# The first gate and up chunk of a SwiGLU taken together, product by product, in a decoder trunk on one core

## The chip, the cores and the metric

The kernel runs on one core of a Trainium2 chip. The metric is the device time of one execution in microseconds (us), lower is better. PE is the matrix engine, DVE the vector engine, ACT the scalar engine, POOL the general engine, SP the engine that issues most DMA transfers. PE has two clock levels, 1.2 and 2.4 GHz.

## The reference, cut to what matters

One decoder layer, float32, 1024 tokens of width 1024, hidden width 2816:

```
x += 1/2 * swiglu(rms_norm(x, ffn1_norm), w_gate, w_up, w_down)     # first FFN
x += mixer(rms_norm(x, mix_norm))                                   # GDN and Mamba heads, not touched
x += 1/2 * swiglu(rms_norm(x, ffn2_norm), w_gate, w_up, w_down)     # second FFN
out = rms_norm(x, final_norm)
swiglu(h) = (silu(h @ w_gate) * (h @ w_up)) @ w_down
```

## The kernel before

**A chunk.** The gate and up matrices are taken in chunks of 256 columns, 11 of each, in the order gate 0, up 0, gate 1, up 1 and so on. One chunk is the product of a 256 by 1024 weight block and the 1024 by 1024 normalised, transposed tokens. It is done by Strassen's scheme in Winograd's form: seven products (numbered 1 to 7) of half-sized operands instead of eight. Every operand is split into a rounded high part and a low rest, so each product is 4 slices of the contraction times three matmuls of 128x512 (L326 high by high, L327 high weights by low tokens, L328 low weights by high tokens): 12 matmuls a product, 84 a chunk.

**Weight operands** (`a_ops`). For each product DVE forms a sum or difference of two blocks (tile `as`, L305; products 3 and 4 need none), ACT rounds it (L235, tile `ah`) and DVE takes the rest (L236, tile `al`). One call makes up to four products into one pair of tiles, of which there are two; a third call waits until every matmul on the first pair has been issued and is done.

**Token operands.** Slices of the normalised tokens are transposed by PE (L212, tile `ps_sc`, two PSUM banks) and combined by DVE and ACT into the operand of each product, again with an ACT cast (L235, tile `bh`) and a DVE rest (L236, tile `bl`). The first 512 tokens (`x0`) give products 2 and 4 (`b_first`). The second 512 (`x1`) with kept copies of the first (`keepx`, called r11 and r21) give 3, 5, 1, 6 and 7 (`b_second`). `b_second` goes slice by slice: for each of four slices it makes all five operands, nine DVE instructions. Temporaries (`bs`, `as`, `raw`, and the copy `m3` of a product) share the tag `q`, four buffers.

**The order of the first two chunks** (`gate_up_all`). Products 2 and 4 of gate 0 and up 0 run first, since their token operands come first. Then the loop over chunks runs gate 0 (3, 5, 1, 7, 6), then up 0, then chunk 2 (gate 1) and so on. PSUM has eight banks: `pj` three, `mx` two, `sc` two, `oo` one. The products' sums are combined on DVE (L375 to L403) and the results written to DRAM (L424).

**What sets the order.** Within an engine the instruction order is fixed when the program is built: a planner goes through the instructions with their data dependences and its own estimate of durations, takes on each engine the earliest instruction in program order that is ready, and so lets later instructions fill gaps. `issue_after(ins)` forces the instructions of a block behind `ins` on that engine. On the chip each engine then runs its list in order.

**The start.** SP issues the first four token blocks (L615), the weight blocks of gate 0 and up 0 (L291) and the last four token blocks (L619). ACT's own DMA queue issues eight small loads of norm and convolution columns (`load_cols`, L96 to L102), which PE transposes and DVE copies into `cols`; the first scaling of tokens (L258) needs them. `normalise_pairs` computes mean squares and scales blocks 0 to 3 in pairs, one square on ACT and one on DVE; `normalise` does blocks 4 to 7 (L164 squares, L166 on the rest, L186 and L188 scaling). At the second FFN the same functions run behind the last output products of the mixer (L121 to L123, L1282).

## Time and profile before

| | |
|---|---|
| time, three runs | 2331.36, 2332.07, 2332.08 us (median 2332.07) |
| the profiled execution | 2332.2 us |
| its span, first to last instruction | 2330.5 us |
| mean granted PE clock | 0.996 |
| PE busy | 2283.3 us (98%) |
| DVE, ACT busy | 1724.9 us (74%), 1100.1 us (47%) |

The profiled execution is 0.1 us above the median of the runs and 1.7 us longer than its span. PE is busy nearly everywhere in the 40 slices of the page; the one low slice is the first (58 us a slice, six tenths). A busy PE can still be one that runs slowly or waits between matmuls, so stretches are read by their instructions.

### The profile page before, as it was taken

What the parts mean: (1) busy time and instruction counts of PE and PEld (TensorE: products, weight loads), DVE (VectorE), ACT (ScalarE), POOL (GpSimd) and SP (SyncE); (2) the same over time, 40 slices, a digit from 0 to 9 for tenths busy, and PEclk for the clock granted to TensorE, in tenths of its full rate; (3) what the DMA queues carried; (4) which work ended last, traced back from release to release, by engine and by line L of the source; (5) the groups of instructions that cost most, each with busy time, mean ns of one, the idle gap of its engine ahead of it and who ended that gap; (6) DMA issues with size and microseconds to landing.
All of it is one profiled execution on the core that took longest, in us unless ns stands there. A gap on an engine that the chain in (4) does not pass through costs nothing.

```text
span 2330.5 us, 31422 instructions
## 1 busy us (share of the span) xinstructions
PE 2283.3 (98%) x11734; PEld 1868.9 (80%) x11734; DVE 1724.9 (74%) x3347; ACT 1100.1 (47%) x1992; POOL 49.5 (2%) x117
## 2 busy tenths in 40 slices
PE   6999999999999999999999999999999999999998
PEld 3788888888878888888888888888778888888886
DVE  7876767667775675668778888778697777767687
ACT  6433333343367785873455556422543333334334
POOL 0000000000000010000000000000000000000000
PEclk9999999999999999999999999999999999999999
DMA  3332323484553322232332322335222333329456
GB/s 110 104 118 88 116 95 109 145 311 131 183 190 107 94 91 55 73 103 73 82 100 73 80 73 64 122 98 190 91 86 95 109 100 109 107 91 348 142 158 214
DMA packets 220967, 281.33 MB, mean 121 GB/s; under 512 B 46905, under 2 KB 153590, under 8 KB 219790
## 3 DMA queue, kind: packets, MB, share of 16 engines
q1 hardware_dynamic: 220548, 279.23, 37.2%
q8 instruction: 92, 1.51, 0.3%
q14 instruction: 61, 0.50, 0.1%
q10 hardware_dynamic: 266, 0.10, 0.0%
HBM read 211.55 MB, written 67.73 MB: 120 GB/s over the span
## 4 chain that ended last, share of the span: by engine, by line
PE 83%; DVE 9%; DMA 3%; ACT 3%; issue 2%; SPq 0%; POOL 0%; ACTq 0%; DVEq 0%
PE ps_pj L123 9%; PE ps_pj L121 9%; PE ps_pj L122 9%; PE ps_pj L327 7%; PE ps_pj L328 6%; PE ps_pj L326 6%; PE ps_mx L326 3%; PE ps_mx L327 3%; PE ps_mx L328 3%; PE ps_pj L485 2%; PE ps_pj L486 2%; PE ps_pj L484 2%; PE ps_oo L327 2%; PE ps_oo L326 2%; PE ps_oo L328 2%
## 5 line engine op out<-in xcount | busy, mean ns | idle before, releaser
L123 PE MATMUL ps_pj<-hhi,wlo 128*128 128x512 f32 x832 | 334.2, 402 | 0.0
L121 PE MATMUL ps_pj<-hhi,whi 128*128 128x512 f32 x832 | 332.9, 400 | 0.4 <-ACT gsb L744 0.4
L122 PE MATMUL ps_pj<-hlo,whi 128*128 128x512 f32 x832 | 332.1, 399 | 0.0
L326 PE MATMUL ps_pj<-bh,ah 128*128 128x512 f32 x704 | 276.0, 393 | 6.8 <-ACT bh L235 6.3
L327 PE MATMUL ps_pj<-bl,ah 128*128 128x512 f32 x704 | 276.8, 393 | 3.7 <-DVE bl L236 3.7
L328 PE MATMUL ps_pj<-bh,al 128*128 128x512 f32 x704 | 275.5, 392 | 0.0
L123 PEld LDWEIGHTS ps_pj<-hhi,wlo 128*128 128x128 f32 x832 | 156.7, 188 | 28.6 <-issue 0.7
L121 PEld LDWEIGHTS ps_pj<-hhi,whi 128*128 128x128 f32 x832 | 156.7, 188 | 28.6 <-ACT gsb L744 0.9
L122 PEld LDWEIGHTS ps_pj<-hlo,whi 128*128 128x128 f32 x832 | 156.7, 188 | 27.9
L326 PEld LDWEIGHTS ps_pj<-bh,ah 128*128 128x128 f32 x704 | 132.5, 189 | 38.8 <-ACT bh L235 11.5
L235 ACT CAST ah<-wst 128x512 fp32r<-128x512 f32 x88 | 54.9, 624 | 226.7 <-PE ps_oo L327 137.6
L327 PEld LDWEIGHTS ps_pj<-bl,ah 128*128 128x128 f32 x704 | 133.0, 189 | 34.5 <-DVE bl L236 7.3
L328 PEld LDWEIGHTS ps_pj<-bh,al 128*128 128x128 f32 x704 | 133.0, 189 | 27.3 <-DVE al L236 0.3
L235 ACT CAST hid<-hraw 128x1024 fp32r<-128x1024 f32 (+1 forms) x84 | 82.4, 983 | 143.1 <-PE ps_oo L486 62.8
L305 DVE TENSOR_TENSOR as<-wst 128x512 f32<-128x512 f32 x220 | 145.3, 685 | 3.7 <-DMA wst<-in_ffn_w_up_dram 2.7
L236 DVE TENSOR_TENSOR al<-as,ah 128x512 fp32r<-128x512 f32 x220 | 140.4, 685 | 0.0
L326 PE MATMUL ps_mx<-bh,ah 128*128 128x512 f32 x352 | 137.5, 393 | 1.7 <-ACT bh L235 1.5
L327 PE MATMUL ps_mx<-bl,ah 128*128 128x512 f32 x352 | 138.3, 393 | 0.7 <-DVE bl L236 0.7
L328 PE MATMUL ps_mx<-bh,al 128*128 128x512 f32 x352 | 137.8, 391 | 0.0
L235 ACT CAST ah<-as 128x512 fp32r<-128x512 f32 x220 | 124.3, 617 | 7.4 <-DVE as L305 7.1
L236 DVE TENSOR_TENSOR hid<-hraw,hid 128x1024 fp32r<-128x1024 f32 (+1 forms) x84 | 95.1, 1132 | 35.0 <-ACT hid L235 34.2
L335 ACT COPY m<-ps_pj 128x512 f32<-128x512 f32 x88 | 51.8, 588 | 129.5 <-PE ps_pj L328 129.5
(427 smaller groups left out, 5086.1 us busy)
## 6 DMA issues: line engine op xcount, KB each, us to landing
hraw<-hid_scr SPq DMA_DIRECT2D x70, 512.0 KB, 3.9
hid_scr<-hs SPq DMA_DIRECT2D x110, 256.0 KB, 2.4
wst<-in_ffn_w_down_dram SPq DMA_DIRECT2D x50, 512.0 KB, 4.7
wst<-in_ffn_w_gate_dram SPq DMA_DIRECT2D x22, 1024.0 KB, 5.6
wst<-in_ffn_w_up_dram SPq DMA_DIRECT2D x22, 1024.0 KB, 5.3
wst<-in_w_in_dram SPq DMA_DIRECT2D x36, 512.0 KB, 4.1
hid_scr<-sg SPq DMA_DIRECT2D x44, 256.0 KB, 2.0
keep<-in_ffn_w_down_dram SPq DMA_DIRECT2D x20, 512.0 KB, 6.2
```

Of the source, the lines that this page charges most:

```text
L121: T.matmul(o, lhsT=wh, rhs=mh, start=first, stop=False)
L122: T.matmul(o, lhsT=wh, rhs=ml, start=False, stop=False)
L123: T.matmul(o, lhsT=wl, rhs=mh, start=False, stop=last)
L235: A.copy(out=hi, in_=src)
L236: return V.tensor_tensor(out=lo, in0=src, in1=hi.bitcast(F32), op=ALU.subtract)
L305: V.tensor_tensor(out=t, in0=v[0], in1=v[1], op=v[2])
L326: T.matmul(bank, lhsT=wh[:, k], rhs=bh[:, k], start=a, stop=False, skip_group_check=True)
L327: T.matmul(bank, lhsT=wh[:, k], rhs=bl[:, k], start=False, stop=False, skip_group_check=True)
L328: T.matmul(bank, lhsT=wl[:, k], rhs=bh[:, k], start=False, stop=z, skip_group_check=True)
L335: A.copy(out=t, in_=bank)
L484: T.matmul(bank, lhsT=hh, rhs=wh, start=first and k == 0, stop=False, skip_group_check=True)
L485: T.matmul(bank, lhsT=hh, rhs=wl, start=False, stop=False, skip_group_check=True)
```

## The change

- `load_cols`: the eight small loads are issued by SP, behind the four token blocks and ahead of the weights, and not by ACT.
- `normalise_pairs`: the square of block 3 is taken on ACT. `a_start(0)` (products 2 and 4 of both chunks) is forced behind the last scaling of the first half on DVE.
- `b_first` no longer makes r21 (the scaled second half of `x0`).
- `a_second` goes. `a_start` makes the weight operands of gate 0 and up 0 together, in four calls: (2, 4), (3, 6), (7, 5), (1), the second one behind `normalise` of the second half.
- `b_second` goes product by product: 3 and 6 for each slice, then 7 (from a second transposing of `x0`), then 5, then 1, with the weight calls 2 and 3 between; r22 is kept.
- `gate_up_all` runs gate 0 and up 0 together: 2 and 4, then 3, 6, 7, 5, 1, each for both chunks, with sums combined in another order; the loop starts at chunk 2. Product 7 takes the two `sc` banks. Weights of gate 1 and up 1 are loaded behind the last weight call.

```diff
     def load_cols(pool):
-        nc.scalar.dma_start(out=st, in_=gdn_conv_w[0].rearrange("t (c p) -> (t c) p", p=P))
+        nc.sync.dma_start(out=st, in_=gdn_conv_w[0].rearrange("t (c p) -> (t c) p", p=P))
...
         for i in range(0, 4, 2):
             ss = pool.tile([P, 2], F32, name="ss")
             A.activation(out=junk[:, 0], in_=xt[i], func=AF.Square, accum_out=ss[:, 0:1])
-            V.scalar_tensor_tensor(out=junk[:, 1], in0=xt[i + 1], scalar=1.0, in1=xt[i + 1],
-                                   op0=ALU.mult, op1=ALU.mult, accum_out=ss[:, 1:2])
+            if i == 0:
+                V.scalar_tensor_tensor(out=junk[:, 1], in0=xt[1], scalar=1.0, in1=xt[1],
+                                       op0=ALU.mult, op1=ALU.mult, accum_out=ss[:, 1:2])
+            else:
+                A.activation(out=junk[:, 1], in_=xt[3], func=AF.Square, accum_out=ss[:, 1:2])
...
-            pt, w1 = transposed(x0, k + 4), wcol[:, k + 4:k + 5]
...
-            A.mul(out=r21[:, k], in_=pt, mul=w1)
...
+    def b_second(pool, x0, x1, wcol, H, r11, r22, between):
...
+        def scaled(pt, kx, other, op):
+            return lambda t: V.scalar_tensor_tensor(out=t, in0=pt, scalar=wcol[:, kx:kx + 1], in1=other,
+                                                    op0=ALU.mult, op1=op)
         for k in range(4):
...
+            A.mul(out=r22[:, k], in_=transposed(x1, k + 4), mul=wcol[:, k + 4:k + 5])
+            p12 = transposed(x1, k)
+            operand(3, k, scaled(p12, k, r22[:, k], ALU.subtract))
+            operand(6, k, scaled(p12, k, r11[:, k], ALU.add))
+        between(2)
+        for k in range(4):
+            operand(7, k, scaled(transposed(x0, k + 4), k + 4, r22[:, k], ALU.add))
+        for k in range(4):
+            split(b_op(H, 5)[0][:, k], b_op(H, 5)[1][:, k], r22[:, k])
+        between(3)
+        for k in range(4):
+            operand(1, k, lambda t: V.tensor_tensor(out=t, in0=r11[:, k], in1=r22[:, k], op=ALU.add))
...
+    A_START = (((0, 2), (0, 4), (1, 2), (1, 4)), ((0, 3), (1, 3), (0, 6), (1, 6)),
+               ((0, 7), (1, 7), (0, 5), (1, 5)), ((0, 1), (1, 1)))
+
+    def a_start(pool, raws, ops, n):
+        a_ops(pool, *((raws[j], m, ops[j]) for j, m in A_START[n]))
...
         for st in ops:
             open_bank(st, "c21", 2, pool.tile([P, 512], F32, name="m2f"))
             prod(st["c21"], st, 4, False)
+        for st in ops:
+            open_bank(st, "c12", 3, pool.tile([P, 512], F32, name="m3", tag="q"))
+        for st, tag in zip(ops, ("pj", "oo")):
+            open_bank(st, "c22", 6, None, tag)
+        for st in ops:
+            open_bank(st, "c11", 7, None, "sc")
...
+        for j, st in enumerate(ops):
+            q, pp = st["m3"], st["m2"]
+            V.tensor_tensor(out=q, in0=q, in1=pp, op=ALU.subtract)
+            V.tensor_tensor(out=pp, in0=st["c21"], in1=q, op=ALU.add)
+            gated(s21, st["c21"], j)
+            V.tensor_tensor(out=pp, in0=st["c11"], in1=pp, op=ALU.add)
+            st["m1"] = wtile(j == 0, "m1")
+            V.tensor_tensor(out=st["m1"], in0=st["c22"], in1=q, op=ALU.add)
+        for j, st in enumerate(ops):
+            prod(st["c12"], st, 5, False)
+            V.tensor_tensor(out=st["m2"], in0=st["m2"], in1=st["c12"], op=ALU.subtract)
+            gated(s12, st["c12"], j)
+        nxt = [{}]
+        for j, st in enumerate(ops):
+            open_bank(st, "c1", 1, None, "mx")
+            pp, r = st["m2"], st["m1"]
+            V.tensor_tensor(out=pp, in0=st["c1"], in1=pp, op=ALU.add)
+            V.tensor_tensor(out=r, in0=st["c1"], in1=r, op=ALU.add)
+            a_ops(pool, *((raws[0], m, nxt[0]) for m in A_GROUPS[j]))
...
+                V.tensor_tensor(out=s11, in0=pp, in1=s11, op=ALU.mult)
+                V.tensor_tensor(out=s22, in0=r, in1=s22, op=ALU.mult)
+                hid_store(work, scr, 0, s12, s22, s11, s21)
+        next_load()
         sg = None
         for i, (p, w) in enumerate(todo):
+            if i < 2:
+                continue
...
+    def start_rest(pool, w_gate, w_up, raws, ops):
+
+        def f(n):
+            a_start(pool, raws, ops, n)
+            if n == 3:
+                raws[:] = [a_load(w, 1) for w in (w_gate, w_up)]
+
+        return f
...
-            x0 = normalise_pairs(npool, xt, "h6")
-            a_first(npool, raws, ops)
-            keep = [kp.tile([P, 4, 512], F32, name=f"keepx{i}") for i in range(2)]
-            b_first(npool, x0, nrm[0], H, keep)
-            a_second(npool, raws, ops)
+            x0, last = normalise_pairs(npool, xt, "h6")
+            with tc.issue_after(last.ins):
+                a_start(npool, raws, ops, 0)
+            r11, r22 = (kp.tile([P, 4, 512], F32, name=f"keepx{i}") for i in range(2))
+            b_first(npool, x0, nrm[0], H, r11)
             x1 = normalise(1, npool, xt, jtag="h7")
-            b_second(npool, x1, nrm[0], H, keep)
+            a_start(npool, raws, ops, 1)
+            b_second(npool, x0, x1, nrm[0], H, r11, r22,
+                     start_rest(npool, ffn1_w_gate[0], ffn1_w_up[0], raws, ops))
...
-    a_first(npool, raws, ops)
-    a_second(npool, raws, ops)
+    a_start(npool, raws, ops, 0)
+    a_start(npool, raws, ops, 1)
...
-    b_second(npool, x1, nrm[2], H, keep)
+    b_second(npool, x0, x1, nrm[2], H, r11, r22, start_rest(npool, ffn2_w_gate[0], ffn2_w_up[0], raws, ops))
```

## Rows read from the trace of the kernel before

**Rows 1.** The page of the whole execution: busy time, share of the span and instructions of each engine; then the shares of the span by engine in the chain that ended last.

```profile
PE 2283.3 (98%) x11734; PEld 1868.9 (80%) x11734; DVE 1724.9 (74%) x3347; ACT 1100.1 (47%) x1992; POOL 49.5 (2%) x117
...
PE 83%; DVE 9%; DMA 3%; ACT 3%; issue 2%; SPq 0%; POOL 0%; ACTq 0%; DVEq 0%
```

**Rows 2.** Busy time of each engine in stretches around the second half of the token operands and behind it: stretch and length, then busy us (instructions) of PE, PEld, DVE, ACT, POOL, granted PE clock, DMA share, GB/s. The first two rows are the first FFN, the third is its steady run of chunks, the last is the second FFN.

```profile
41.30:63.70 22.40, 15.79 (x62) 9.21 (x60) 21.66 (x36) 14.81 (x26) 0.00 (x0) 0.92 0.00 1
63.70:86.12 22.42, 22.42 (x99) 18.43 (x99) 21.91 (x37) 12.47 (x21) 0.00 (x0) 1.00 0.36 118
104.00:150.00 46.00, 46.00 (x204) 38.10 (x203) 32.09 (x52) 15.93 (x29) 0.00 (x0) 1.00 0.33 109
1692.90:1706.55 13.65, 9.62 (x30) 5.17 (x28) 13.65 (x23) 9.26 (x16) 0.00 (x0) 0.72 0.00 0
```

**Rows 3.** PE's instructions in order of time: start, duration, line, output and inputs, shape, count, and in brackets the idle time before it and what ended it. The first matmul of the first FFN, the last one that waited in its first two chunks, the first one of chunk 2 and of chunk 2's product 2; then in the second FFN the first matmul of product 2, the first transposing of `x1`, and the first matmul of chunk 2.

```profile
21.66 1.22 PE L326 MATMUL ps_mx<-bh,ah 128*128 128x512 f32 x2 [0.43 <-ACT bh L235]
...
63.70 0.50 PE L327 MATMUL ps_pj<-bl,ah 128*128 128x512 f32 x1 [0.70 <-DVE bl L236]
...
83.40 0.39 PE L326 MATMUL ps_pj<-bh,ah 128*128 128x512 f32 x1
...
86.12 0.39 PE L326 MATMUL ps_mx<-bh,ah 128*128 128x512 f32 x1
...
1676.58 0.39 PE L326 MATMUL ps_mx<-bh,ah 128*128 128x512 f32 x1
...
1682.14 0.66 PE L212 MATMUL ps_sc<-ident,xt 128*128 128x128 f32 x4 [0.34 <-ACT xt L186]
...
1729.13 0.39 PE L326 MATMUL ps_pj<-bh,ah 128*128 128x512 f32 x1
```

**Rows 4.** DVE's instructions in order of time, same columns: the first of `b_second` and the first combining of sums behind it, in the first and in the second FFN.

```profile
42.03 0.75 DVE L279 SCALAR_TENSOR_TENSOR bs<-ps_sc,cols,raw 128x512 f32<-128x512 f32 x1 [2.08 <-ACT raw L277]
...
64.78 0.68 DVE L375 TENSOR_TENSOR m<-m,m2f 128x512 f32<-128x512 f32 x1
...
1684.46 0.75 DVE L279 SCALAR_TENSOR_TENSOR bs<-ps_sc,cols,raw 128x512 f32<-128x512 f32 x1 [2.12 <-ACT raw L277]
...
1706.59 0.69 DVE L375 TENSOR_TENSOR m<-m,m2f 128x512 f32<-128x512 f32 x1
```

**Rows 5.** The start: two rows of what SP's queue waited for (us in total, times, longest), the first and the last of the eight column loads on ACT's queue, SP's issue of gate 0's weights, ACT's first instruction, and PE's transposing of the last columns.

```profile
SPq L615 <- DMA xt<-in_x_dram: 3.0, 1, 3.0
SPq L615 <- DMA colst<-in_ssm_conv_b_dram: 1.1, 1, 1.1
...
0.81 0.42 ACTq L96 DMA_DIRECT2D colst<-in_gdn_conv_w_dram  x1
...
5.69 0.28 ACTq L102 DMA_DIRECT2D colst<-in_ffn_norm_dram  x1
...
6.54 0.43 SPq L291 DMA_DIRECT2D wst<-in_ffn_w_gate_dram  x1
...
6.00 1.28 ACT L197 ACT_TABLE_LOAD   x1 [6.00 <-DMA colst<-in_ssm_conv_w_dram]
...
8.46 0.39 PE L105 MATMUL ps_mx<-ident,colst 93*128 93x93 f32 x1 [3.41 <-DMA colst<-in_ffn_norm_dram]
```

**Rows 6.** Busy time of each engine in stretches of the start, columns as in rows 2.

```profile
12.00:21.00 9.00, 3.36 (x12) 1.98 (x12) 8.30 (x23) 5.46 (x9) 0.00 (x0) 1.00 1.00 362
...
21.00:28.00 7.00, 6.57 (x27) 5.22 (x26) 3.46 (x6) 6.36 (x13) 0.00 (x0) 1.00 0.01 4
28.00:34.00 6.00, 4.29 (x20) 2.52 (x18) 5.06 (x9) 6.00 (x13) 0.00 (x0) 1.00 0.01 1
```

**Rows 7.** DVE and ACT in order of time, first FFN: the square of block 1, first and last step of the first pair's inverse root, the square of block 3, the first weight cast, the scaling of block 2, the first scaling by a column, the first square of the second half and the start of its inverse root.

```profile
5.99 1.23 DVE L198 SCALAR_TENSOR_TENSOR junk<-xt 128x1024 bf16<-128x1024 f32 x1 [5.99 <-DMA xt<-in_x_dram]
...
8.47 0.17 DVE L201 TENSOR_SCALAR ssv<-ss 128x2 f32<-128x2 f32 x1 [1.25 <-ACT junk L197]
...
10.60 0.15 DVE L118 SCALAR_TENSOR_TENSOR rstd<-rs_t,rstd 128x2 f32<-128x2 f32 x1
...
11.24 1.23 DVE L198 SCALAR_TENSOR_TENSOR junk<-xt 128x1024 bf16<-128x1024 f32 x1 [0.50 <-DMA xt<-in_x_dram]
...
14.38 0.62 ACT L235 CAST ah<-wst 128x512 fp32r<-128x512 f32 x1 [2.46 <-DMA wst<-in_ffn_w_gate_dram]
...
17.30 1.15 ACT L204 ACTIVATE xt<-xt,rstd 128x1024 f32<-128x1024 f32 x1 [1.04 <-DVE rstd L118]
...
19.38 0.68 ACT L258 ACTIVATE keepx<-ps_sc,cols 128x512 f32<-128x512 f32 x1
19.96 1.04 ACT L164 ACTIVATE junk<-xt 128x1024 bf16<-128x1024 f32 x1
...
36.34 0.17 DVE L166 TENSOR_SCALAR ssv<-ss 128x4 f32<-128x4 f32 x1
```

**Rows 8.** One transposing of four blocks on PE, and the three steps of one operand of product 7 (DVE sum, ACT cast, DVE rest), first FFN, columns as in rows 3.

```profile
57.35 0.60 PE L212 MATMUL ps_sc<-ident,xt 128*128 128x128 f32 x4
57.44 0.68 DVE L285 TENSOR_TENSOR bs<-keepx,raw 128x512 f32<-128x512 f32 x1
...
58.20 0.61 ACT L235 CAST bh<-bs 128x512 fp32r<-128x512 f32 x1
...
59.30 0.68 DVE L236 TENSOR_TENSOR bl<-bs,bh 128x512 fp32r<-128x512 f32 x1
```

More of the change, by code (lines that the diff above doesn't have):

```diff
@@ L252, in b_op, with b_first @@
         return H[m]
-    def b_first(pool, x0, wcol, H, keep):
-        r11, r21 = keep
+    def b_first(pool, x0, wcol, H, r11):
         for k in range(4):
@@ L259, in b_first @@
             split(b_op(H, 2)[0][:, k], b_op(H, 2)[1][:, k], r11[:, k])
-            pt, w1 = transposed(x0, k + 4), wcol[:, k + 4:k + 5]
             t = pool.tile([P, 512], F32, name="bs4", tag="q")
-            V.scalar_tensor_tensor(out=t, in0=pt, scalar=w1, in1=r11[:, k], op0=ALU.mult, op1=ALU.subtract)
+            V.scalar_tensor_tensor(out=t, in0=transposed(x0, k + 4), scalar=wcol[:, k + 4:k + 5],
+                                   in1=r11[:, k], op0=ALU.mult, op1=ALU.subtract)
             split(b_op(H, 4)[0][:, k], b_op(H, 4)[1][:, k], t)
-            A.mul(out=r21[:, k], in_=pt, mul=w1)
-    def b_second(pool, x1, wcol, H, keep):
-        r11, r21 = keep
+    def b_second(pool, x0, x1, wcol, H, r11, r22, between):
         def operand(m, k, f):
@@ L308, in a_ops @@
             ops[m] = hi[:, i], lo[:, i]
-    def a_first(pool, raws, ops):
-        a_ops(pool, *((raws[j], m, ops[j]) for j in range(2) for m in (2, 4)))
-    def a_second(pool, raws, ops):
-        a_ops(pool, *((raws[0], m, ops[0]) for m in (3, 5, 1, 7)))
+    A_START = (((0, 2), (0, 4), (1, 2), (1, 4)), ((0, 3), (1, 3), (0, 6), (1, 6)),
+               ((0, 7), (1, 7), (0, 5), (1, 5)), ((0, 1), (1, 1)))
+    def a_start(pool, raws, ops, n):
+        a_ops(pool, *((raws[j], m, ops[j]) for j, m in A_START[n]))
     def gate_up_all(pool, H, w_gate, w_up, scr, raws, ops, work, tail):
         todo = [(p, w) for p in range(NF2) for w in (w_gate, w_up)]
-        loads = todo[2:]
+        loads = todo[4:]
         def prod(bank, ops, m, first):
@@ L336, in open_bank, with wtile, next_load @@
                 st[f"m{m}"] = t
-        nxt = ops
+        def wtile(gate, name):
+            return work.tile([P, 512], F32, name=name, tag="sg" if gate else "mu", bufs=8 if gate else 3)
+        def next_load():
+            raws.pop(0)
+            if loads:
+                pn, wn = loads.pop(0)
+                raws.append(a_load(wn, pn))
         for st in ops:
@@ L341, in gate_up_all, with gated @@
             prod(st["c21"], st, 4, False)
+        for st in ops:
[4 more added lines that the diff above has]
+            open_bank(st, "c11", 7, None, "sc")
+        s12, s21 = (wtile(True, name) for name in ("sg12", "sg21"))
+        def gated(o, bank, j):
+            if j == 0:
+                A.activation(out=o, in_=bank, func=AF.Silu)
+            else:
+                V.tensor_tensor(out=o, in0=bank, in1=o, op=ALU.mult)
@@ L358, in prep @@
                     tail.pop(0)()
-                if raws and (i == 0 or grp == 1):
-                    raws.pop(0)
-                    if loads:
-                        pn, wn = loads.pop(0)
-                        raws.append(a_load(wn, pn))
+                if raws and grp == 1:
+                    next_load()
             def wt(name):
-                return work.tile([P, 512], F32, name=name, tag="sg" if gate else "mu", bufs=8 if gate else 3)
+                return wtile(gate, name)
             open_bank(st, "c12", 3, pool.tile([P, 512], F32, name="m3", tag="q"))
-            if i == 0:
-                prod(st["c12"], st, 5, False)
-            if i > 1:
-                open_bank(st, "c21", 2, wt("m2"))
+            open_bank(st, "c21", 2, wt("m2"))
             open_bank(st, "c11", 1, wt("m1"))
@@ L1323 @@
             x0 = normalise(0, npool, xt2, jtag="h6")
-            keep = [natp.tile([P, 4, 512], F32, name="keepx", tag=t) for t in ("nat", "zg")]
-            b_first(npool, x0, nrm[2], H, keep)
+            r11, r22 = (natp.tile([P, 4, 512], F32, name="keepx", tag=t) for t in ("nat", "zg"))
+            b_first(npool, x0, nrm[2], H, r11)
     x1 = normalise(1, npool, xt2, jtag="h7")
-    b_second(npool, x1, nrm[2], H, keep)
+    b_second(npool, x0, x1, nrm[2], H, r11, r22, start_rest(npool, ffn2_w_gate[0], ffn2_w_up[0], raws, ops))
     c2.close()
```

47 lines of the change are left out of this document (18 added, 29 removed).

## The prediction

> **What bounds the kernel now.** I read the page's totals and chain first: PE is busy for 98% of the span and carries 83% of the chain, DVE 9% [rows 1]. PE's work is hardly changed, so a gain can only come from where PE waits. The waits of PE by stretch stand at the start of each FFN: in the steady run of chunks PE is busy for 46.0 of 46.0 us and DVE for 32.1 (70%), but while the second half of the token operands is made DVE is busy for 21.7 of 22.4 us and 13.65 of 13.65, PE starves between, and the granted clock is 0.92 and 0.72 [rows 2]. In order of time, DVE enters `b_second` at 42.03 and leaves it at 64.78; PE's last wait on a token rest ends at 63.70, and from there PE runs without a gap into chunk 2 at 83.40 [rows 3, 4]. In the second FFN the same is 1684.46 to 1706.59, chunk 2 at 1729.13. So the measure of the change is when chunk 2 starts, twice; behind it the kernel is the same.
>
> **How starved.** Twelve matmuls from 83.40 lie 2.72 us before the next product at 86.12, 0.227 each [rows 3]; two chunks are 168, or 38.1 us. The first FFN takes 61.7 us for them (21.66 to 83.40). With 16 transposings at 0.37 us (their row shows 0.60 [rows 8], but the next matmul starts while they drain; an estimate) that is 44, so some 17 us are lost there. In the second FFN 24 of the 168 are done between 1676.58 and 1682.14; 144 matmuls (32.6) and 8 transposings (3.0) stand against 47.0 us: 11.4 lost.
>
> **The cost of a DVE instruction.** `b_second` and one weight rest are 37 instructions in 22.75 us (42.03 to 64.78), and 36 in 22.13 in the second FFN: 0.615 us each, back to back [rows 4].
>
> **Order by product: what DVE must do before chunk 2.** Counted in the diff, from the first operand of product 3: 16 for products 3 and 6 (sum and rest, four slices), 8 for the weights of 7 and 5, 8 for the tokens of 7, 4 rests for 5, 4 for the weights of 1, 8 for the tokens of 1: 48. The sums behind them are 12, two more for the first product 1, and one rest before chunk 2's first product is whole: 63. At 0.615 that is 38.7 us, if DVE never waits. The old order needs the same sums, but hands PE gate 0 alone, so PE starts up 0 after DVE is through. New instructions are few: four transposings of `x0` per FFN, done a second time, cost PE 1.5 us, hidden as PE waits there; product 7's sum now reads PSUM (0.75 as L279 [rows 4] for 0.68 [rows 8]), 4 times 0.07. The r21 scalings go, four on ACT per FFN, as long as L258's 0.68 [rows 7].
>
> **Does PE keep up?** Products 3 and 6 give PE 12 matmuls (2.7 us) per slice against four DVE instructions (2.5). Product 7 is late: it needs the `sc` banks that its own four transposings use, so both chunks wait for the last of them to be read, instruction 31 or so, 19 us in; then 72 matmuls (16.3 us) follow: 35.5 us from the first operand, under DVE's 38.7. So DVE sets chunk 2. Behind it DVE has the rest of the pair (20 instructions), chunk 2's six and one rest for chunk 3, 27 or 16.6 us, while PE takes 19.0 for chunk 2: no second stall. The weight loads of gate 1 are issued after instruction 40 (24.6 us), 14 us before use; gate 0's block took 7.8 us from issue to use (6.54 to 14.38) with the transfer engines full [rows 5 to 7]. The weight tiles: call 3 needs products 3 and 6 done, call 2 products 2 and 4; DVE arrives later than PE in both FFNs.
>
> **Second FFN.** The first operand stays at 1684.46, as `x1` waits for the mixer's output products, and weight call 1 has room before (DVE has gaps there). 1684.46 + 38.7 = 1723.2 against 1729.13: 5.9 us gained. PE alone would reach 1682.14 + 32.6 + 12 times 0.37 = 1719.2, a bound of 9.9. Lower bound: nothing gained, if DVE waits 6 us.
>
> **First FFN, the head.** SP issued the third and fourth token block late: it waited 3.0 us for a block and 1.1 us for a column load [rows 5]. With the columns behind, four issues of some 0.4 us are through by 2.5 us. At 362 GB/s [rows 6] a block of 512 KB takes 1.4 us; the second block was there at 5.99, so the fourth comes near 8.8 and not 11.24, where DVE's wait for it ended [rows 7]. ACT, which waited until 6.00 for a column load before it loaded its table [rows 5], begins earlier too. With both squares on ACT at 10.0, an inverse root of 2.3 us (8.47 to 10.75) and a scaling of 1.15, `x0` is ready at 13.5, where it was 18.45; part of it is that the second root no longer shares DVE with weight operands [rows 7]. The price: eight issues, the first 0.42 and the last 0.28 us [rows 5], the last few held until the token blocks land, put the weights about 2.6 us later (issued near 9.1, not 6.54), so gate 0's land near 17 (14.38 before) and the last token block near 23.6 (transfers filled the engines until 21 before [rows 6]). The columns must be there at 14: the last was transposed 2.8 us behind its issue (5.69 to 8.46), so about 11.8 now, in time.
>
> The Trainium skill ("Trainium Kernel Development and Optimization", Key Constraints) says that transfers of SP, ACT and POOL share the same 16 engines and that several issuing engines save issue time alone. By that the move would only cost: the fourth block would not come 2.4 us earlier and the sum would be 2319.4. The trace differs: what held SP was two waits for landings, 4.1 us, not issues.
>
> From 13.5 ACT has 7.2 us of `b_first` (per slice a scaling, 0.58 from its start to the next, and two casts of 0.61), four weight casts (2.4) and four squares of `x1` (1.04 and a readout, 1.2 each, 4.9): 28.0. ACT is the bound there, as before (12.36 of 13.0 us in 21 to 34 [rows 6]). From the second half's root to DVE's first operand it took 42.03 - 36.34 = 5.7 us [rows 4, 7]: 33.7. DVE in the meantime has 24 instructions, the root and two scalings, some 18.4 of the 20 us, so of weight call 1 (6 instructions, 3.7 us) I leave half behind: 1.8. Chunk 2 then starts at 33.7 + 1.8 + 38.7 = 74.2 instead of 83.40: 9.2 us. Bounds: at best PE binds: first matmul at 18.2 (17 and a sum and a cast), 38.1 + 19 transposings 7.0 + 1.6 for the slow first ones (two took 1.22 [rows 3]; an estimate) = 64.9, a gain of 18.5. At worst DVE idles 5.2 us more, as it did between 12 and 34 [rows 6], and call 1 stands behind whole: 33.7 + 3.7 + 38.7 + 5.2 = 81.3, a gain of 2.1.
>
> **Sum.** 9.2 + 5.9 = 15.1 us off the profiled 2332.2 (0.1 above the median): 2317.1, given as 2317. With both worst bounds it is 2330, with both best 2303.8.
>
> **Rivals.**
> - *DVE waits inside the pair.* The two `m3` copies hold two of the four `q` buffers until product 6 is summed, so some 14 operands per FFN (weights of 7 and 5, tokens of 7, weights and tokens of 1) pass through two. A pass is 0.68 + 0.61 + 0.68 = 2.0 us at least [rows 8], 1.0 per operand with two buffers, against 1.23 of DVE work: no wait if the order is perfect. At 1.5 us an operand, 28 times 0.27 = 7.6: 2324.6. The planner, which orders by estimates, speaks for it; DVE's 13.65 of 13.65 with all four buffers [rows 2] against it.
> - *Slower.* The same place with one buffer left, because another temporary holds the second: 2.0 us an operand, 28 times 0.77 = 21.6: 2338.6. It turns slower than before at 15.1 / 28 + 1.23 = 1.77 us an operand. Against it: two buffers are free by the count.
> - *The clock.* In the second FFN PE, fed by halves, was granted 0.72 over 13.65 us, that is some 7.6 us at 1.2 GHz. If PE's wait for product 7 (about 8 us in the first FFN) brings the same in both and PE binds, 3.8 us each: 2324.6. The steadier feed of products 3 and 6 speaks against it. The Trainium skill ("TensorE: Matmul & The Clock Gate", Part 1) holds the throttled level to be the default, which activity releases; the 0.72 agrees.
> - *PE binds.* If the planner puts sums late and DVE waits nowhere: 2332.2 - 18.5 - 9.9 = 2303.8.
>
> **How the numbers follow.** Forecast (2308 to 2323) 0.65; DVE waits 0.18; clock 0.06; slower 0.08; PE binds 0.03. The prediction is the first, 2317. The range reaches to the other cases on both sides, 2306 to 2327. A measurement of this kernel tells about 0.2%, 4.7 us, from no change. Faster by more: 0.64 + 0.14 + 0.04 + 0.03 = 0.85; same 0.07, from the edges; slower 0.08.
>
> **What would show it.** After the change: `x0`'s scaling ending near 13.5 and not 18.5; the first matmul near 18; DVE's first operand near 34; chunk 2's first matmul near 74, and near 1723; PE idle before product 7; no waits of PE in chunk 2. Wrong would make it: DVE idle between operands with ACT or a buffer named, weights of gate 0 far behind 17, PE waiting at chunk 2 or 3 for weight operands, or a granted clock near half between 35 and 75.

## The result and the profile after

| | before | changed |
|---|---|---|
| median | 2331.45 us (2328.24 to 2332.08, 6 runs) | 2318.28 us (2316.70 to 2320.04, 6 runs) |
| ratio | | 0.9947, 95% interval 0.9934 to 0.9960 |
| profiled execution, span | 2332.2, 2330.5 us | 2316.89, 2315.2 us |

The forecast was 2317 us. The changed kernel was measured twice more, beside other runs of the kernel before: 2317.45 and 2317.94 against 2330.28 both times. So the gain is 12 to 13 us. How it is made up differs from the forecast's sum, and the rest of this document is about that.

The page of the changed kernel, totals and chain, answers [rows 1]: PE's 98% stays, and DVE's share of the chain goes from 9% to 6%.

```profile
PE 2276.3 (98%) x11766; PEld 1869.5 (81%) x11766; DVE 1724.7 (74%) x3349; ACT 1093.0 (47%) x1982; POOL 49.6 (2%) x117
...
PE 88%; DVE 6%; ACT 3%; DMA 2%; issue 1%; SPq 0%; POOL 0%; DVEq 0%; ACTq 0%
```

PE in order of time (start, duration, line, output and inputs, count, and in brackets the idle time before and what ended it) answers [rows 3]: the first matmul, PE's two waits inside the pair, chunk 2; then the second FFN's first transposing of `x1`, its wait inside the pair, and its chunk 2. In the new file L331 to L333 are the three matmuls, L340 the copy of a product, L215 the transposing.

```profile
20.00 0.79 PE L331 MATMUL ps_mx<-bh,ah 128*128 128x512 f32 x1 [0.43 <-ACT ah L238]
...
57.69 0.47 PE L331 MATMUL ps_sc<-bh,ah 128*128 128x512 f32 x1 [1.90 <-DVE bs L275]
...
66.61 0.80 PE L331 MATMUL ps_pj<-bh,ah 128*128 128x512 f32 x1 [3.20 <-ACT m L340]
...
79.23 0.39 PE L331 MATMUL ps_pj<-bh,ah 128*128 128x512 f32 x1
...
1672.96 0.66 PE L215 MATMUL ps_sc<-ident,xt 128*128 128x128 f32 x4 [0.34 <-ACT xt L186]
...
1703.29 0.50 PE L331 MATMUL ps_pj<-bh,ah 128*128 128x512 f32 x1 [1.97 <-ACT m L340]
...
1714.30 0.39 PE L331 MATMUL ps_pj<-bh,ah 128*128 128x512 f32 x1
```

DVE in order of time, same columns, answers [rows 4]: its first operand of product 3, the first sum, the rest of chunk 2's first weights (L239); then in the second FFN the first operand and the rest of chunk 2's first weights.

```profile
38.66 1.41 DVE L275 SCALAR_TENSOR_TENSOR bs<-ps_sc,cols,keepx 128x512 f32<-128x512 f32 x2 [2.02 <-ACT keepx L279]
...
68.35 1.29 DVE L372 TENSOR_TENSOR m<-m,m2f 128x512 f32<-128x512 f32 x2
...
75.24 0.68 DVE L239 TENSOR_TENSOR al<-wst,ah 128x512 fp32r<-128x512 f32 x1
...
1675.29 1.41 DVE L275 SCALAR_TENSOR_TENSOR bs<-ps_sc,cols,keepx 128x512 f32<-128x512 f32 x2 [2.11 <-ACT keepx L279]
...
1713.58 0.68 DVE L239 TENSOR_TENSOR al<-wst,ah 128x512 fp32r<-128x512 f32 x1
```

Three things are to be read here. Chunk 2 of the first FFN starts at 79.23, a gain of 4.2 us where 9.2 were forecast. In the second FFN the time from the first `x1` transposing to chunk 2 is 41.34 us instead of 46.99: 5.65, forecast 5.9. And PE's longest wait in each pair (3.20 and 1.97 us) names ACT's copy of product 3 (L340), not a DVE operand; the 1.90 us in the first pair are the wait for product 7's bank, which DVE reads. The remaining 5.0 us between these two traces lie between chunk 2 of the first FFN and the first `x1` transposing of the second, in code that wasn't changed: 1593.73 us, where the kernel before had 1682.14 - 83.40 = 1598.74.

The stretches of the pair (columns as in [rows 2]) show DVE full and PE slowed: 5.39 us of PE in eight at a granted clock of 0.79, then PE full. The last row is the second FFN's pair, at full clock all through, where [rows 2] had 0.72.

```profile
56.00:64.00 8.00, 5.73 (x24) 4.43 (x24) 8.00 (x14) 3.01 (x5) 0.00 (x0) 1.00 0.09 16
64.00:72.00 8.00, 5.39 (x17) 4.33 (x18) 8.00 (x14) 4.30 (x7) 0.00 (x0) 0.79 0.75 249
72.00:79.00 7.00, 7.00 (x32) 5.80 (x31) 6.60 (x12) 3.00 (x6) 0.00 (x0) 1.00 0.20 75
...
1674.70:1714.20 39.50, 37.53 (x184) 30.37 (x183) 38.83 (x64) 21.46 (x37) 0.00 (x0) 1.00 0.20 63
```

### The profile page after: what moved, and what is told of

The parts are those of the page before. It is cut to its first block, busy times and chain, and to the rows that moved or that the text cites. A ratio compares the mean times of both kernels' runs of the same rounds, so it can differ in the third digit from the quotient of the medians.

```text
span 2315.2 us, 31468 instructions
## 1 busy us (share of the span) xinstructions
PE 2276.3 (98%) x11766; PEld 1869.5 (81%) x11766; DVE 1724.7 (74%) x3349; ACT 1093.0 (47%) x1982; POOL 49.6 (2%) x117
## 4 chain that ended last, share of the span: by engine, by line
PE 88%; DVE 6%; ACT 3%; DMA 2%; issue 1%; SPq 0%; POOL 0%; DVEq 0%; ACTq 0%
PE ps_pj L123 10%; PE ps_pj L121 10%; PE ps_pj L122 10%; PE ps_pj L331 6%; PE ps_pj L332 6%; PE ps_pj L333 6%; PE ps_mx L331 3%; PE ps_mx L333 3%; PE ps_mx L332 3%; PE ps_pj L531 2%; PE ps_pj L532 2%; PE ps_pj L530 2%; PE ps_oo L331 2%; PE ps_oo L333 1%; PE ps_oo L332 1%
## 5 line engine op out<-in xcount | busy, mean ns | idle before, releaser
L331 PE MATMUL ps_pj<-bh,ah 128*128 128x512 f32 x680 | 265.4, 391 | 5.2 <-ACT m L340 5.2
L332 PE MATMUL ps_pj<-bl,ah 128*128 128x512 f32 x680 | 265.3, 390 | 0.0
L333 PE MATMUL ps_pj<-bh,al 128*128 128x512 f32 x680 | 265.1, 390 | 0.0
L121 PEld LDWEIGHTS ps_pj<-hhi,whi 128*128 128x128 f32 x832 | 156.7, 188 | 28.6 <-ACT gsb L801 0.8
L123 PEld LDWEIGHTS ps_pj<-hhi,wlo 128*128 128x128 f32 x832 | 156.7, 188 | 28.6 <-issue 0.7
L331 PEld LDWEIGHTS ps_pj<-bh,ah 128*128 128x128 f32 x680 | 127.8, 188 | 32.3 <-ACT m L340 6.0
L333 PEld LDWEIGHTS ps_pj<-bh,al 128*128 128x128 f32 x680 | 128.1, 188 | 26.9
L332 PEld LDWEIGHTS ps_pj<-bl,ah 128*128 128x128 f32 x680 | 128.0, 188 | 26.3
L331 PE MATMUL ps_mx<-bh,ah 128*128 128x512 f32 x368 | 144.4, 393 | 1.7 <-ACT bh L238 1.1
L332 PE MATMUL ps_mx<-bl,ah 128*128 128x512 f32 x368 | 144.0, 391 | 0.0
L333 PE MATMUL ps_mx<-bh,al 128*128 128x512 f32 x368 | 143.8, 391 | 0.1
L239 DVE TENSOR_TENSOR al<-as,ah 128x512 fp32r<-128x512 f32 x220 | 140.2, 684 | 0.2
L239 DVE TENSOR_TENSOR hid<-hraw,hid 128x1024 fp32r<-128x1024 f32 (+1 forms) x84 | 95.0, 1131 | 32.8 <-ACT hid L238 32.4
L239 DVE TENSOR_TENSOR al<-wst,ah 128x512 fp32r<-128x512 f32 x88 | 60.6, 689 | 67.0 <-ACT ah L238 66.9
```

Source lines behind the costliest of these rows:

```text
L121: T.matmul(o, lhsT=wh, rhs=mh, start=first, stop=False)
L123: T.matmul(o, lhsT=wl, rhs=mh, start=False, stop=last)
L239: return V.tensor_tensor(out=lo, in0=src, in1=hi.bitcast(F32), op=ALU.subtract)
L331: T.matmul(bank, lhsT=wh[:, k], rhs=bh[:, k], start=a, stop=False, skip_group_check=True)
L332: T.matmul(bank, lhsT=wh[:, k], rhs=bl[:, k], start=False, stop=False, skip_group_check=True)
L333: T.matmul(bank, lhsT=wl[:, k], rhs=bh[:, k], start=False, stop=z, skip_group_check=True)
```

## The experiments

Times are medians. "First operand" is the start of DVE's first operand of product 3 in the first FFN. "Pair 2" is the time from that operand to chunk 2 in the second FFN. "Middle" goes from chunk 2 of the first FFN to the first `x1` transposing of the second. All but the medians come from one trace each.

| kernel | median us | ratio to before, 95% interval | first operand | chunk 2 | middle | pair 2 |
|---|---|---|---|---|---|---|
| before (profiled 2332.2) | 2330.09 to 2331.45 | | 42.03 | 83.40 | 1598.7 | 44.7 |
| changed | 2318.28 | 0.9947, 0.9934 to 0.9960 | 38.66 | 79.23 | 1593.7 | 39.0 |
| ffn1_only | 2324.07 | 0.9974, 0.9964 to 0.9983 | 38.44 | 79.01 | 1593.6 | 45.6 |
| ffn2_only | 2325.06 | 0.9977, 0.9967 to 0.9986 | 43.42 | 84.81 | 1594.9 | 40.6 |
| order_only | 2317.41 | 0.9945, 0.9929 to 0.9962 | 38.54 | 79.06 | 1595.1 | 39.0 |
| head_only | 2333.36 | 1.0011, 1.0001 to 1.0020 | 41.08 | 86.96 | 1597.8 | 45.5 |
| cols_pool | 2318.14 | 0.9949, 0.9936 to 0.9961 | 37.32 | 77.83 | 1593.2 | 39.0 |
| m3_work | 2319.20 | 0.9958, 0.9944 to 0.9971 | 39.08 | 78.57 | 1594.0 | 41.8 |
| both | 2319.06 | 0.9950, 0.9937 to 0.9962 | 37.17 | 75.00 | 1593.1 | 41.7 |
| changed_again | 2317.45 | 0.9948, 0.9935 to 0.9960 | 39.05 | 78.27 | 1594.1 | 39.0 |
| m3_first | 2315.89 | 0.9935, 0.9922 to 0.9947 | 37.94 | 77.36 | 1592.9 | 40.7 |
| m3_first_sq | 2315.09 | 0.9931, 0.9918 to 0.9945 | 37.81 | 77.15 | 1595.3 | 39.0 |
| changed_third | 2317.94 | 0.9943, 0.9930 to 0.9955 | 39.09 | 78.29 | 1593.7 | 39.0 |

### The two FFNs apart: ffn1_only and ffn2_only

Edit: one FFN as in the changed kernel, the other with the functions of before kept beside the new ones.

```
-    b_second(npool, x0, x1, nrm[2], H, r11, r22, start_rest(...))     # ffn1_only: second FFN
+    b_second_old(npool, x1, nrm[2], H, keep)
```

> The first FFN as in the changed kernel, the second as before. Theory A, the two FFN starts are where the gain arises and what lies between (5.0 us less from chunk 2 of the first FFN to the first transposing of x1 in the second) is variation of the execution or of the planner's order: chunk 2 starts near 79.2 us and the time falls by 4 us, to about 2327.5. Theory B, a changed first FFN also makes the unchanged middle 5 us shorter: the time falls by 9 us, to about 2322.5. My forecast had 9.2 us in the first FFN alone.

> The first FFN as before, the second as in the changed kernel. Both theories: from the first transposing of x1 to chunk 2 41.3 us (47.0 before), so 5.7 us less, about 2326. If the middle's 5 us is variation that any execution can show, the first transposing of x1 may come well before 1682 here too, with an unchanged first FFN; if it comes from the changed first FFN, it stays at 1682 within 1 us.

Against 2330.09, the first FFN alone takes 6.0 us off and the second alone 5.0, together 11.0 of the 12 to 13. So neither half carries the result, and the first one gives about half, not the 9.2 of 15.1 that the sum had. ffn1_only's time lies between theories A and B, nearer to B. But ffn2_only speaks for A's variation: its first `x1` transposing comes at 1679.74, well before 1682.14, behind a first FFN in the code of before. That first FFN varies too: it starts chunk 2 at 84.81 here and at 83.40 in the trace of before. The granted clock stood at half for 3.4 us twice (from 34.3 and from 51.3) where before's stood there once (from 50.3).

### Head and order apart: order_only and head_only

Edits: the changed kernel with the head of before (columns on ACT's queue, block 3's square on DVE, weights not forced behind the scaling); and the kernel before with these three edits alone.

```
-            x0, last = normalise_pairs(npool, xt, "h6")               # order_only
-            with tc.issue_after(last.ins):
-                a_start(npool, raws, ops, 0)
+            x0 = normalise_pairs(npool, xt, "h6")
+            a_start(npool, raws, ops, 0)
```

> As changed, but the head of the first FFN as before: columns on ACT's queue, one square on DVE, no forced order. Theory W, the later weights (17.8 instead of 14.4 us) eat what the earlier tokens give: DVE's first operand of product 3 comes at 38.7 us or up to 1.5 us earlier, chunk 2 at 78 to 79.5, time as changed. Theory H, the head's edits are worth what x0 gains (15.0 instead of 18.5 us): the first operand comes near 41.5, chunk 2 near 82, time 2.8 us above the changed kernel.

> The kernel before with the head's edits alone: columns on SP, the square of block 3 on ACT, the first weight operands forced behind the last scaling. Theory H: x0 ready at 15.0, DVE's first instruction of b_second 3 us earlier (39), chunk 2 at 80.4, time 2329. Theory W: weights usable at 17.8, that instruction within 1 us of 42.0, time within 1 us of before.

The new order with the old head is as fast as the changed kernel. Its `x0` comes 3.8 us later, and DVE's first operand all the same at 38.54. The rows are ACT's first weight cast, the last scaling of `x0` and the last square of `x1`, then the start of the second half's root on DVE and the operand:

```profile
14.80 0.62 ACT L235 CAST ah<-wst 128x512 fp32r<-128x512 f32 x1 [2.80 <-DMA wst<-in_ffn_w_gate_dram]
...
17.70 1.15 ACT L204 ACTIVATE xt<-xt,rstd 128x1024 f32<-128x1024 f32 x1 [1.04 <-DVE rstd L118]
...
28.32 1.05 ACT L164 ACTIVATE junk<-xt 128x1024 bf16<-128x1024 f32 x1
...
29.83 0.17 DVE L166 TENSOR_SCALAR ssv<-ss 128x4 f32<-128x4 f32 x1
...
38.54 1.41 DVE L272 SCALAR_TENSOR_TENSOR bs<-ps_sc,cols,keepx 128x512 f32<-128x512 f32 x2 [2.03 <-ACT keepx L276]
```

These are theory W's numbers, but not for its reason: the weights weren't late, as the next section shows. With the old head ACT casts gate 0's weights while `x0` isn't ready, and is through with the squares of `x1` at 29.5, where the changed kernel is at 32.0. DVE then puts six other instructions inside the root, which ends at 35.1 in both.

The head alone gains nothing either: `x0` starts its last scaling at 13.65 and DVE its first operand 0.95 us earlier, but chunk 2 comes 3.6 us later. The granted clock goes with that: it stood at half for 10.2 us between 54.4 and 68.1, and for 3.4 us in before. In the same ten microseconds, before and then with the head edits:

```profile
60.00:70.00 10.00, 8.71 (x34) 6.26 (x35) 10.00 (x17) 5.69 (x10) 0.00 (x0) 1.00 0.26 81
```

```profile
60.00:70.00 10.00, 9.04 (x25) 6.51 (x26) 10.00 (x17) 6.04 (x9) 0.00 (x0) 0.66 0.33 105
```

PE is busier in the second row and does 25 matmuls instead of 34. The other executions lean the same way: the mean clock of the ten lies between 0.992 and 0.996, that of the 25 of before beside them between 0.994 and 0.997, most at 0.996. Neither theory had the time, 3.3 us above before. So the head edits, which the sum counted as part of 9.2 us, are worth nothing as they stand.

### What held the head: cols_pool

Edit: the eight column loads on POOL's queue.

```
-        nc.sync.dma_start(out=st, in_=gdn_conv_w[0].rearrange("t (c p) -> (t c) p", p=P))
+        nc.gpsimd.dma_start(out=st, in_=gdn_conv_w[0].rearrange("t (c p) -> (t c) p", p=P))
```

> The changed kernel, with the eight column loads issued on POOL's queue, so that SP goes from the token blocks straight to the weights. Theory W (the head lost its gain to the late weights): gate 0's weights usable near 14.5 us instead of 17.8, DVE's first operand of product 3 near 35.5 instead of 38.66, chunk 2 of the first FFN near 76 instead of 79.23, and the time about 3 us under the changed kernel's. Rival S (the sum of ACT's work up to the second half's operands sets it, since order_only came to 38.54 with the old head): first operand within 1 us of 38.6, chunk 2 within 1 us of 79.2, and the time within 1 us of the changed kernel's.

First the changed kernel: SP's issues of the last two columns and of gate 0's weights, and the stretch from 8.20 to 10.40 (columns as in [rows 2], the last two being DMA share and GB/s).

```profile
7.20 0.27 SPq L102 DMA_DIRECT2D colst<-in_mix_norm_dram  x1
8.60 0.27 SPq L102 DMA_DIRECT2D colst<-in_ffn_norm_dram  x1
8.91 0.41 SPq L296 DMA_DIRECT2D wst<-in_ffn_w_gate_dram  x1
...
8.20:10.40 2.20, 0.40 (x1) 0.18 (x1) 1.75 (x8) 1.18 (x3) 0.00 (x0) 1.00 0.16 22
```

The last three column loads were each held until a token block had landed, 3.1 us together, and the weights stood behind them. When they were issued at last, the token blocks were through: the transfer engines moved 22 GB/s for 2.2 us.

But 17.8, which the theories take for the time when gate 0's weights were usable, is only their first use. In the changed kernel, the start of `x0`'s last scaling on ACT, a token rest and the first weight sum on DVE, the first weight cast and the last square on ACT, and the root:

```profile
13.89 1.15 ACT L207 ACTIVATE xt<-xt,rstd 128x1024 f32<-128x1024 f32 x1 [2.26 <-DVE rstd L118]
...
17.19 0.69 DVE L239 TENSOR_TENSOR bl<-keepx,bh 128x512 fp32r<-128x512 f32 x1 [2.34 <-ACT bh L238]
17.80 0.69 DVE L310 TENSOR_TENSOR as<-wst 128x512 f32<-128x512 f32 x1
...
18.30 0.61 ACT L238 CAST ah<-wst 128x512 fp32r<-128x512 f32 x1
...
30.90 1.06 ACT L164 ACTIVATE junk<-xt 128x1024 bf16<-128x1024 f32 x1
...
32.08 0.17 DVE L166 TENSOR_SCALAR ssv<-ss 128x4 f32<-128x4 f32 x1 [0.69 <-ACT junk L164]
```

No row waits for the load. By the trace's record of its semaphore it was complete at 14.52, and at 14.36 in the kernel before: the moved columns cost the weights 0.2 us. What stood ahead of them were the lists of the engines. DVE's has a token rest ahead of the first weight sum, and that rest waited 2.3 us for ACT; ACT's has two scalings by a column and a token cast ahead of the first weight cast. In order_only and cols_pool ACT casts gate 0 as it lands (14.80 behind 14.77, 12.71 behind 12.69). The planner made these lists; the estimates it made them by are not on record.

With the columns on POOL's queue the weights go at 2.67 and the hole is filled:

```profile
2.67 0.55 SPq L296 DMA_DIRECT2D wst<-in_ffn_w_gate_dram  x1
...
8.20:10.40 2.20, 0.00 (x0) 0.00 (x0) 1.56 (x6) 2.04 (x3) 0.00 (x0) 1.00 1.06 358
...
12.71 0.62 ACT L238 CAST ah<-wst 128x512 fp32r<-128x512 f32 x1 [1.12 <-DMA wst<-in_ffn_w_gate_dram]
...
29.30 0.17 DVE L166 TENSOR_SCALAR ssv<-ss 128x4 f32<-128x4 f32 x1
...
37.32 1.41 DVE L275 SCALAR_TENSOR_TENSOR bs<-ps_sc,cols,keepx 128x512 f32<-128x512 f32 x2 [3.46 <-ACT keepx L279]
```

The weights land at 12.7 instead of 14.5 and are cast at once, and the root of the second half starts at 29.30 instead of 32.08. How much of these 2.8 us is the earlier load and how much the other order on ACT isn't separated. Only 1.3 of them reach the first operand. On the way stands PE:

```profile
30.82 0.50 PE L331 MATMUL ps_mx<-bh,ah 128*128 128x512 f32 x1 [3.13 <-ACT m2f L340]
...
31.55 0.63 PE L333 MATMUL ps_mx<-bh,al 128*128 128x512 f32 x1
31.98 0.63 PE L331 MATMUL ps_mx<-bh,ah 128*128 128x512 f32 x1
...
35.05 0.60 PE L215 MATMUL ps_sc<-ident,xt 128*128 128x128 f32 x4
```

PE waited 3.1 us for ACT's copy of product 2, which stood behind squares and casts; then it ran product 4 with matmuls 0.43 apart (half clock, 0.23 at full), and the transposings of `x1` stood behind those matmuls on PE. The first operand and chunk 2 (37.32 and 77.83) lie between W's numbers and S's. The load did land 1.8 us later through SP's queue, but the head has other limits, the lists and PE. The median doesn't move (2318.14, and 2317.45 for the changed kernel measured beside it).

### What held PE in the pair: m3_work, both, m3_first

Edit of m3_work: the copies of product 3 in buffers of another pool. `both` adds it to cols_pool; m3_first is `both` with the edit in the first FFN alone.

```
-            open_bank(st, "c12", 3, pool.tile([P, 512], F32, name="m3", tag="q"))
+            open_bank(st, "c12", 3, work.tile([P, 512], F32, name="m3", tag="hs", bufs=5))
```

> The changed kernel, with the copies of product 3 in the two chunks of the pair kept in buffers of the work pool instead of q buffers, so that they need not wait for a q buffer. Theory C (PE's 3.2 us wait at 66.61 is the copy of product 3 that came late for want of a q buffer): the wait goes, chunk 2 of the first FFN starts at 75.9 to 77.5 instead of 79.23, the second FFN stays within 1 us (DVE bound: 39.0 us from first operand to chunk 2), and the time is 2 to 3.5 us under the changed kernel's. Rival D (DVE is full from 46 to 72 us, and the wait only moves to the token operands of product 1): chunk 2 within 1 us of 79.2, the time within 1 us.

> Both of the two edits, columns on POOL's queue and the copies of product 3 in the work pool. If W and C hold and add, chunk 2 of the first FFN starts at 73 to 74 us and the time is about 2312.5. If S and D hold, chunk 2 stays at 79 and the time at 2318. If only one holds, it is that one's result.

> The changed kernel with the columns on POOL's queue, and the copies of product 3 in the work pool in the first FFN alone; the second FFN is the changed kernel's. Theory (two late things, the weights and the copy, cost the first FFN its gain, and the second FFN is best as changed): chunk 2 of the first FFN at 75.0 us as in the kernel with both edits, the second FFN 39.0 us from DVE's first operand to chunk 2 instead of 41.7, span about 2.7 us under that kernel's 2313.4, so near 2311; median about 3 us under the changed kernel's. Rival (what the first FFN gains is given back behind it, or is less than a median of runs can tell): chunk 2 near 75, but the median within 1.5 us of the changed kernel's.

PE's waits from 40 to 90 us (us in total, times, longest), in the changed kernel and then in `both`:

```profile
PE ps_pj L331 <- ACT m L340: 3.2, 1, 3.2
PE ps_sc L331 <- DVE bs L275: 1.9, 1, 1.9
```

```profile
PE ps_mx L331 <- ACT sg L366: 3.2, 1, 3.2
PE ps_pj L331 <- ACT m L340: 0.3, 1, 0.3
```

In the changed kernel ACT copies product 3 at 65.98 and 67.50, among the casts of the last token operand; in `both` at 54.43:

```profile
65.98 0.58 ACT L340 COPY m<-ps_pj 128x512 f32<-128x512 f32 x1
```

```profile
54.43 1.07 ACT L340 COPY m<-ps_pj 128x512 f32<-128x512 f32 x2 [0.23 <-PE ps_sc L215]
```

So for the first FFN the `q` buffers were the cause: with buffers of their own the copies come 11.6 us earlier in ACT's list, and the wait goes. A wait of the same length comes up behind it, at the PSUM bank of product 1, which DVE's sums and a SiLU have to free first. That one follows DVE, and chunk 2 follows it by 24 matmuls: 37.17 to 75.00 is 37.8 us (forecast 38.7), where the changed kernel took 40.6. That 75.00 is nearly the forecast 74.2 is in part luck. The first operand came 1.7 us later than forecast, and of the four traces with this edit `both` is the only one whose clock stayed up behind the new wait. In m3_work, m3_first and m3_first_sq eight matmuls run at half clock there, and the same way takes 39.3 to 39.5 us. In m3_work that leaves chunk 2 at 78.57: the wait shrinks to 0.5 us, as theory C had it, and the number is rival D's.

In the second FFN the same edit costs 2.7 us (41.7 and 41.8 for 39.0). In m3_work the first copy comes there at 1703.42, 28.6 us behind the first operand; in the changed kernel at 1702.65, 27.4 behind it. Both times it stands behind token casts in ACT's list, so the `q` buffers aren't what holds it in that FFN; the order on ACT is. PE's wait for it is 3.1 us instead of 2.0, and the rest of the 2.7 us is half clock on eight matmuls behind it, in both traces. That is why m3_work and `both` don't gain in the median. The 2315.23 of `both`'s profiled execution is the lowest of its five; 2312.5 was forecast if both theories add, and the median is 2319.06.

m3_first has the first FFN's code of `both`, and PE waits as long at product 1. It reaches chunk 2 at 77.36 all the same. First `both`, then m3_first:

```profile
69.39 0.50 PE L331 MATMUL ps_mx<-bh,ah 128*128 128x512 f32 x1 [3.16 <-ACT sg L366]
...
75.00 0.39 PE L331 MATMUL ps_pj<-bh,ah 128*128 128x512 f32 x1
```

```profile
70.16 0.76 PE L331 MATMUL ps_mx<-bh,ah 128*128 128x512 f32 x1 [3.17 <-ACT sg L367]
70.72 0.63 PE L332 MATMUL ps_mx<-bl,ah 128*128 128x512 f32 x1
71.14 0.63 PE L333 MATMUL ps_mx<-bh,al 128*128 128x512 f32 x1
...
77.36 0.39 PE L331 MATMUL ps_pj<-bh,ah 128*128 128x512 f32 x1
```

The 24 matmuls of product 1 take 5.6 us there and 7.2 here, the first eight at 1.2 GHz. After the same wait the clock was down in one execution and not in the other. (The other 0.8 us came in at the first operand.) Its second FFN shows the same: 40.7 us for 39.0, at a mean clock of 0.97 between 1660 and 1720 instead of 1.00. Neither the theory nor its rival had 77.36. The median of m3_first is 2315.89, 2 us under the changed kernel beside it (3 expected), with intervals that overlap.

### One more edit of the head, and the changed kernel again

m3_first_sq forces the squares of blocks 2 and 3 ahead of the first scaling on ACT:

```
+        sq = A.activation(out=junk[:, 1], in_=xt[3], func=AF.Square, accum_out=sums[1][:, 1:2])
...
-            A.mul(out=xt[i], in_=xt[i], mul=r[:, 0:1])
+            with tc.issue_after(sq.ins):
+                A.mul(out=xt[i], in_=xt[i], mul=r[:, 0:1])
```

> As m3_first, with the squares of blocks 2 and 3 forced ahead of the first scaling on ACT. If the start of the first FFN is set by x0's readiness, x0's last scaling starts about 1 us earlier than 13.8, the second half's root and DVE's first operand come up to 1 us earlier, and chunk 2 at 74 instead of 75. If ACT's sum of work or PE's order sets it, chunk 2 stays within 0.5 us of 75.

> The changed kernel once more, for the unchanged stretch between chunk 2 of the first FFN and the first transposing of x1 in the second FFN: 1593.7 us in the changed kernel's trace and 1598.7 in that of before. If the 5.0 us are the order that the planner gives to that stretch, this execution shows 1593.7 within 1 us; if they are variation from execution to execution, it may lie up to 4 us off.

> The changed kernel on the same chip as the two above, for their comparison: 2316 to 2319, and chunk 2 of the first FFN at 78.3 to 79.2 as in its two traces.

The squares bring `x0` 0.3 us forward (13.36 for m3_first's 13.68) and little behind it: chunk 2 is at 77.15 for 77.36. The kernel has the lowest median of all, 2315.09, but its interval overlaps that of the changed kernel beside it; the intervals alone don't rank the two.

The middle of the changed kernel is 1593.7, 1594.1 and 1593.7 in its three traces, as the planner's order would have it. But the order isn't the cause. In the mixer, ffn1_only has the instructions of PE, DVE and ACT in the very order of before (6040, 1800 and 1135 of them, by their tiles), and takes 987.7 us from the first projection to the last output product, where before takes 989.4. Of the 5.0 us, 1.5 lie in front of the mixer's first transposing: there PE waits 2.07 us in before and 0.71 in changed, but 2.23 in order_only, which has the new first FFN. Another 1.5 lie right behind it, where the clock of before stood at half (657.9 to 661.3). The last 1.9 are the mixer's. Two other kernels have long mixers too, head_only (989.6) and m3_first_sq (989.2, with the new first FFN); each is 1.5 us longer in one part, and there, in this order, the clock is down:

```profile
861.00:869.00 8.00, 7.85 (x38) 6.76 (x39) 5.96 (x11) 6.26 (x9) 0.45 (x1) 0.79 0.02 6
```

```profile
850.00:858.00 8.00, 8.00 (x37) 6.70 (x37) 6.77 (x11) 5.71 (x9) 1.43 (x1) 0.79 0.07 11
```

ffn2_only (989.2) is 1.4 us longer in another part, in which PE waits 1.1 us more, for a transfer. So the middle varies from trace to trace with waits and clock, and that the change makes it shorter isn't shown.

## Why the prediction was right, and where it wasn't

**The measure.** In the two traces chunk 2 starts 4.2 and 5.65 us earlier, 9.9 together, and 12 to 13 were measured. Single traces don't fix these terms to the microsecond. The first FFN of before starts chunk 2 at 83.40 or 84.81, the changed one at 78.27 to 79.23; from the first `x1` transposing to chunk 2 the second FFN of before takes 47.0 to 47.9 us, the changed one 41.3 to 41.4 where the clock stays up and 42.9 in ffn2_only, where it falls. So the two pairs may give all of the gain, or leave 2 to 3 us to the middle; that isn't settled. The sum also started from a profiled time that was 2 us above the later medians. By the median of ffn1_only the first FFN is worth 6.0 us, not 9.2, and that 2317 came out all the same is in part luck.

**Second FFN.** Right: 63 DVE instructions at 0.615, 38.7 us from the first operand to chunk 2, measured 39.0 in the traces where the clock stayed up. DVE was full (38.83 of 39.5 us) and had chunk 2's rest done at 1714.26. PE came to chunk 2 at the same time: behind its 1.97 us wait it ran 48 matmuls without a gap to 1714.30. So the number is right, and the trace doesn't tell which of the two sets it.

**DVE's cost and its waits.** Right in the first FFN too: DVE reached chunk 2's first weight rest at 75.24 and had it done at 75.9, 37.3 us behind the first operand, with two sums of product 1 still to come, and it didn't wait between operands.

**The mis-sized term: 9.2 us for the first FFN, measured 4.2.** It has two parts, 3.2 us ahead of the first operand (38.66 for 35.5) and 1.9 behind it (40.6 for 38.7).
- *Ahead.* The failing step is "28.0", the end of ACT's work before the root: 32.08. Of these 4.1 us, 1.5 are `x0`, ready at 15.04 (13.89 and 1.15) and not at 13.5, since block 3's square stood behind the first scaling on ACT. Three ACT instructions ahead of the root aren't in the sum, two casts of product 3's weights and a copy of product 2, 1.5 us. And ACT was idle for 1.9 us where the sum has no gap: 1.3 for PE's transposings, 0.6 for a weight sum of DVE. What the sum did count took some 0.8 less, by difference. Gate 0's weights didn't hold it: they landed at 14.52, before "near 17". order_only shows that `x0` alone doesn't set the end: 3.8 us on `x0` moved the first operand by 0.1, as ACT did other work meanwhile. The 1.8 us put down for leftover weight operands fell inside the root instead, which took 3.1 us for 2.2 that way.
- *Behind.* "The two `m3` copies hold two of the four `q` buffers" had it the wrong way round in the first FFN. The copies came last, and PE waited for them: 3.2 us at 66.61, just before it would have caught up. PE then ran the next product's first matmuls at half clock. Its time adds up: product 7 started 19.0 us behind the first operand, as forecast; 72 matmuls are 16.3, the wait is 3.2, and eight matmuls at half clock cost 1.7, which is 40.2 of the 40.6. So PE, late, set chunk 2 and not DVE. In `both`, with the copy in time, PE's last wait follows DVE again, and it is 37.8 us.

**The price of the moved columns.** Put at 2.6 us on the weights, it was 0.2 (landed at 14.52 for 14.36): the token blocks ahead of them were through at 8.58 instead of 11.22. What the held loads cost shows only against cols_pool, where gate 0 lands at 12.69. The Trainium skill ("Trainium Kernel Development and Optimization", Key Constraints) has several issuing engines save issue time alone. Here they did more: held issues on SP's queue let the transfer share fall to 0.16 for 2.2 us, and on POOL's queue it stayed at 1.06. In the median neither move is worth anything. The earlier `x0` that the prediction took the page to deny was there (15.04 for 18.45) and was lost later; the 3.3 us by which head_only is slower go with the clock and are no price of the queue.

**The clock.** It was a rival with 0.06 as something that the new feeding might bring. In the second FFN it went the other way, from 0.72 to 1.00 in the changed kernel. In the first pair or the second, though, every trace of the changed kernel and its variants has such a stretch, as before's has one from 50.3: a granted clock of 0.79 over eight microseconds is some 3.4 us at 1.2 GHz, ahead of one of PE's waits or behind it. In the changed kernel's first trace that stretch lies in 64 to 72, behind the wait, and costs. In changed_again (and in changed_third) it lies in 56 to 64, ahead of it:

```profile
56.00:64.00 8.00, 6.10 (x21) 4.76 (x20) 8.00 (x15) 3.08 (x6) 0.00 (x0) 0.79 0.05 6
```

The wait shrinks there from 3.2 to 1.6 and chunk 2 is 1.0 us earlier.

**Open.** What decides in one execution that the clock falls after a wait and in another that it doesn't isn't settled. Nor is why the planner put gate 0's weights 3.3 us behind their landing, nor whether the middle gives any of the gain.

## What to carry to other kernels

An earlier operand is worth something only if the next thing its consumers need is early too: count ahead of a stage along each engine's list, with the last input of each instruction, not by adding up the busy engine's instructions. An instruction that starts late on a loaded tile need not have waited for the load; look for a row that waits for it, or for the landing itself, before the queue is blamed. Before small loads are put in front of large ones on a queue, ask whether they will be held there by earlier landings; here that was 1.8 us on the large one, and nothing in the time. And where two users share a tag of buffers, work out which one the scheduler serves first: the one that is served last may be the one that the bounding engine waits for. Last, a difference of a few microseconds between two single traces is no effect of the change until other traces show it.
